# Routing that finds the group first and the two experts by a search of the eight largest, g2 spread by DMAs, and rms factors by one GpSimd power

## The chip, the core and the metric

The kernel runs on one core of a Trainium2 chip. The core has TensorE (PE in the profile; its weight loads are PEld), VectorE (DVE), ScalarE (ACT), GpSimd (POOL) and SyncE (SP), which issues most of the DMAs. Every engine works through its own queue of instructions in order. Data lie in HBM, in SBUF (128 partitions) and, for the results of TensorE, in PSUM. The metric is device time in microseconds (us), as the median of several runs; the profile is one further execution.

## What is computed

Two transformer blocks on 256 tokens of width 1024, in float32. The change lies in the first block's mixture of experts and in the factor of every rms norm; the second block (latent attention, gated linear attention, memory attention, a feed-forward part) it touches through that factor alone.

```python
def rms_norm(x, eps=NORM_EPS):
    y = xf * lax.rsqrt(jnp.mean(xf * xf, axis=-1, keepdims=True) + eps)

def hier_moe(h, w_group, b_group, w_router, b_router, w13, w2):
    """Top-1 expert group, then top-2 SwiGLU experts within it. h (b, s, d)."""
    g_logits = (hf @ w_group + b_group).astype(jnp.float32)
    g_prob = jax.nn.softmax(g_logits, axis=-1)
    p_g, g_idx = lax.top_k(g_prob, 1)
    e_logits = (hf @ w_router + b_router)....reshape(T, N_EXPERT_GROUPS, EXPERTS_PER_GROUP)
    within = jnp.take_along_axis(e_logits, g_idx[:, :, None], axis=1)[:, 0]
    top_v, top_i = lax.top_k(within, TOP_K)
    gate = p_g * jax.nn.softmax(top_v, axis=-1)
    expert_id = (g_idx * EXPERTS_PER_GROUP + top_i).astype(jnp.int32)
    ...   # y = sum over the token's two experts of gate * (silu(a) * b) @ w2[e], [a, b] = h @ w13[e]

sh1, sc1, g1, sh2, sc2, g2 = jnp.split(silu(c) @ w_ada + b_ada, 6, axis=-1)
x = x + g1 * mixer(modulate(x, sh1, sc1))
x = x + g2 * hier_moe(modulate(x, sh2, sc2))   # modulate: rms_norm(x) * (1 + scale) + shift
```

There are 4 groups of 8 experts, each with w13 of 1024x1024 and w2 of 512x1024, 6 MB of float32 weights an expert.

## The kernel before

Block 1's first part (`phase_a`) keeps the state transposed, xT, features on partitions. `ada_part` makes the 48 modulation columns `mod` in three parts of four weight loads each: four matmuls with 32 equal columns leave the result on four groups of 32 partitions, a copy takes it to `ada`, and four transposes turn it. `mod[:, 40:48]` is g2 as columns. At the end of the mixer, features 0 to 7 of x1T (the sum x + g1·mix, in tiles of 128) are made one after the other, squared on ScalarE and added up on VectorE; two matmuls with a column of ones give the tokens' sums `ss`, `rsqrt_cols` makes r2 of it, and L is the 36 router logits times r2 plus a bias.

`rsqrt` (lines 123 to 136) computes v^-0.5 on VectorE: a bit shift and an integer operation for a first guess, v times -0.5, and three Newton steps of three operations (L133 to L135); with the sum's scaling (L120) 13 operations at a site. Thirteen sites call it.

`routing` is a generator. Its first part transposes x1T into token rows (L695, tiles mm), scales them by r2 on ScalarE as `tm` and rounded as `h2h` (L699, L700), subtracts on GpSimd for the rest `h2l` (L701), and has `moe_start` put x1T into the four PSUM tiles of the result by sixteen transposes (L882). Then VectorE searches: `first_max` (L713 to L719) finds the first largest of the last axis, for all four groups at once (128x64), once more with the first one masked out (wi), and over the four groups (128x8); M (128x2x32, L733) marks a token's two experts. Matmuls with M give the experts' counts and ranks: pc (L736, L738) and, with a triangle and ones, the ranks of four experts (`ranks`, L744 to L747). Two groups of four matmuls (L757) and two copies on ScalarE (L760) spread g2 over all 128 partitions as `g2row`. The later parts of the generator, run under the first pass, transpose M (L768), sort the experts by their counts into P (L772 to L784), bring M, the counts and the gates G into that order (L788 to L792, L836 to L843), and compute the gates (L810 to L832).

`phase_b` goes through 32 experts in 11 passes: six with two experts, five with four. For two passes at a time `onehot` (L1003) makes the selecting matrix from the ranks, `gather` (L910) collects h2's rows by matmuls with h2h and h2l, and VectorE (L916) and ScalarE (L919) apply scale sc2 and shift sh2. `experts` then does w13 in eight k steps (L937, two PSUM tiles pa and pb), the gate by tanh and two products (L962 to L964), transposes (L967), w2 (L977), and adds the result, times gate and g2row (L984), to the result's tiles (L991). In the first pass a step of `routing` runs after each k step from the third on. The transposes of oh and matmuls with G (L948, L950) stand behind the k steps. Weights come by SP into ring buffers (`ring`, 2 MB) and `xb`; a buffer is given back when its matmuls are done (`done`), and SP's next load into it waits for that. The first four experts' weights do not depend on the routing.

Large matmuls of the other parts are done in three products of rounded halves: ScalarE rounds a weight (whi, L111), VectorE or GpSimd subtracts for the rest (wlo, L115 and L113).

The order on PE, DVE, ACT and POOL is that of a scheduler that goes through the program with a model of time; `tc.issue_after(x)` holds what follows behind instruction x. SP's order is that of the code.

## Time and profile before

| | |
|---|---|
| median of 3 runs | 1133.19 us (lowest 1131.82) |
| profiled execution | 1135.8 us, span 1134.0 us |
| busy share of the span | PE 93%, DVE 49%, ACT 39%, POOL 17% |
| HBM read | 324.57 MB, 287 GB/s over the span |

A row of the timeline gives start and duration in us, the engine, the line, the operation, output <- inputs by the program's names (numbers left out), partitions x elements, and the count of equal neighbours; behind it in brackets the engine's idle time ahead of it and what ended it. A group row gives busy us and mean ns of one, then idle time ahead and its releasers. A row of the waits gives total us, times and longest. A PE row often counts two records for one float32 matmul. The granted clock of PE is a share of 2.4 GHz.

### The profile page before, as it was taken

Reading aid. Unit: us, or ns where it says so; the run is one execution under the profiler, and the core shown is the slowest. Engines: PE = TensorE matmul, PEld = TensorE weight load, DVE = VectorE, ACT = ScalarE, POOL = GpSimd, SP = SyncE. Lnnn points to the kernel's source line nnn. Section 1 sums busy time; section 2 is a strip of 40 time slices with the busy share of each in tenths; the row PEclk is TensorE's granted clock in tenths of the full one; section 3 lists DMA queues with packets and bytes.
Section 4 is the critical chain, followed back from the end, with each engine's and each line's share of the span. In section 5 each row is a group of like instructions: output and inputs, shape, how many; then the busy total and the mean of one; then the engine's idle time right before and its main releaser. Section 6 shows DMA issues by size and latency. Waiting matters only on the chain. (4 is left out here: it accounts for less than half of the span.)

```text
span 1134.0 us, 18448 instructions
## 1 busy us (share of the span) xinstructions
PE 1055.1 (93%) x6921; PEld 714.0 (63%) x6921; DVE 554.7 (49%) x1355; ACT 436.7 (39%) x982; POOL 189.3 (17%) x181
## 2 busy tenths in 40 slices
PE   4999998999999998877889999999999999999998
PEld 2677778534343332241224578888898888898997
DVE  4498756312121220020211588475896766664664
ACT  3354434101111120010101557566864555565653
POOL 1453112000000000000001432222111132222221
PEclk9999989899999999979999999999999999999999
DMA  9885669499999999999999844553442243554531
GB/s 369 331 334 222 274 260 387 159 419 388 421 421 419 420 374 422 421 417 421 421 420 421 333 159 151 214 186 124 177 150 75 75 167 140 214 205 167 223 149 38
DMA packets 36279, 314.38 MB, mean 277 GB/s; under 512 B 4160, under 2 KB 4672, under 8 KB 5328
## 3 DMA queue, kind: packets, MB, share of 16 engines
q1 hardware_dynamic: 36176, 313.05, 69.0%
q8 instruction: 59, 0.97, 0.3%
q14 instruction: 44, 0.36, 0.1%
HBM read 324.57 MB, written 1.05 MB: 287 GB/s over the span
## 5 line engine op out<-in xcount | busy, mean ns | idle before, releaser
L111 ACT ACTIVATE whi<-ring 128x512 fp32r<-128x512 f32 (+3 forms) x378 | 228.6, 613 | 194.4 <-PE mm L175 94.6
L115 DVE TENSOR_TENSOR wlo<-ring,whi 128x512 fp32r<-128x512 f32 (+3 forms) x262 | 185.6, 711 | 131.6 <-ACT whi L111 119.8
L113 POOL TENSOR_TENSOR wlo<-ring,whi 128x512 fp32r<-128x512 f32 (+2 forms) x116 | 152.3, 1317 | 495.7 <-ACT whi L111 469.4
L937 PE MATMUL pb<-xb,xT 128*32 128x512 f32 x736 | 132.9, 595 | 7.4 <-DMA xb<-w 7.4
L937 PE MATMUL pb<-ring,xT 128*32 128x512 f32 x672 | 119.5, 595 | 5.3 <-DMA ring<-w 5.3
L963 DVE SCALAR_TENSOR_TENSOR g<-g,pb 128x256 f32<-128x256 f32 x22 | 9.3, 421 | 169.3 <-ACT g L962 169.3
L977 PE MATMUL pb<-xb,hT 128*32 128x512 f32 x464 | 84.8, 630 | 3.2 <-DMA xb<-w 2.7
L937 PEld LDWEIGHTS pb<-xb,xT 128*32 128x32 f32 x736 | 36.4, 109 | 81.0 <-issue 59.0
L962 ACT ACTIVATE g<-pb 128x256 f32<-128x256 f32 x22 | 8.4, 384 | 173.9 <-PE pb L937 168.6
L175 PE MATMUL mm<-h_lo,whi 128*128 128x256 f32 (+1 forms) x264 | 75.4, 286 | 0.0
L174 PE MATMUL mm<-h_hi,whi 128*128 128x256 f32 (+1 forms) x264 | 75.1, 285 | 0.0
L176 PE MATMUL mm<-h_hi,wlo 128*128 128x256 f32 (+1 forms) x264 | 75.1, 285 | 0.0
L113 POOL TENSOR_TENSOR ml<-ring,mh 128x256 fp32r<-128x256 f32 x8 | 5.6, 726 | 400.1 <-ACT mh L111 400.1
L175 PE MATMUL mm<-xg_lo,whi 128*128 128x256 f32 x256 | 71.2, 280 | 0.9 <-DVE xg_lo L1115 0.9
L174 PE MATMUL mm<-xg_hi,whi 128*128 128x256 f32 x256 | 70.7, 280 | 0.6 <-DVE xg_lo L1115 0.6
L176 PE MATMUL mm<-xg_hi,wlo 128*128 128x256 f32 x256 | 70.9, 279 | 0.0
L937 PEld LDWEIGHTS pb<-ring,xT 128*32 128x32 f32 x672 | 29.3, 109 | 65.0 <-issue 48.3
L984 DVE SCALAR_TENSOR_TENSOR Y<-pb,gs,g2row 128x512 f32<-128x512 f32 x22 | 16.5, 749 | 85.7 <-PE pb L977 84.8
L187 PE MATMUL mm<-whi,h_hi 128*128 128x512 f32 (+2 forms) x144 | 53.3, 374 | 0.6 <-issue 0.5
L188 PE MATMUL mm<-whi,h_lo 128*128 128x512 f32 (+2 forms) x144 | 53.3, 372 | 0.0
L977 PE MATMUL pb<-ring,hT 128*32 128x512 f32 x240 | 49.2, 618 | 3.4 <-ACT hT L968 1.9
L977 PEld LDWEIGHTS pb<-xb,hT 128*32 128x32 f32 x464 | 21.3, 114 | 48.4 <-issue 37.6
(530 smaller groups left out, 2245.3 us busy)
## 6 DMA issues: line engine op xcount, KB each, us to landing
xb<-w SPq DMA_DIRECT2D x110, 1024.0 KB, 15.6
ring<-w SPq DMA_DIRECT2D x82, 1024.0 KB, 13.3
ring<-w_in SPq DMA_DIRECT2D x18, 2048.0 KB, 8.4
ring<-w_ada SPq DMA_DIRECT2D x12, 2048.0 KB, 13.4
ring<-w_up SPq DMA_DIRECT2D x8, 2048.0 KB, 7.4
ring<-w_down SPq DMA_DIRECT2D x8, 2048.0 KB
ring<-w_out SPq DMA_DIRECT2D x2, 2048.0 KB, 11.9
ring<-w_mem_kv SPq DMA_DIRECT2D x2, 2048.0 KB
```

Source lines behind the costliest of these rows:

```text
L111: self.nc.scalar.activation(hi, src, AF.Copy)
L113: self.nc.gpsimd.tensor_tensor(out=lo, in0=src, in1=hi.bitcast(F32), op=OP.subtract)
L115: self.nc.vector.tensor_tensor(out=lo, in0=src, in1=hi.bitcast(F32), op=OP.subtract)
L174: nc.tensor.matmul(out, hv[:, k], xh[:, k0 + k], start=f, stop=False)
L175: nc.tensor.matmul(out, hv[:, k], xl[:, k0 + k], start=False, stop=False)
L176: nc.tensor.matmul(out, lv[:, k], xh[:, k0 + k], start=False, stop=l)
L187: nc.tensor.matmul(out[t], xh[:, k, s], hv[:, 0], start=f, stop=False)
L188: nc.tensor.matmul(out[t], xl[:, k, s], hv[:, 0], start=False, stop=False)
L937: nc.tensor.matmul(q[r, :], x[:, k, r], w[side[i]][:, h * 512:h * 512 + 512], start=k == 0, stop=k == KT - 1)
L963: nc.vector.scalar_tensor_tensor(g[:, r], g[:, r], 1.0, pa[:, r], op0=OP.add, op1=OP.mult)
L977: nc.tensor.matmul(y[h][r, :], hT[:, f * 128 + i * 32:f * 128 + i * 32 + 32], w[side[i]][:, h * 512:h * 512 + 512], start=f == 0, stop=f == 3)
L984: nc.vector.scalar_tensor_tensor(Y, y[h], gs, self.g2row[:, h * 512:h * 512 + 512], op0=OP.mult, op1=OP.mult)
```

## The change

Six parts. (1) `rsqrt` is one GpSimd power with a column of -0.5. (2) g2row: the bias part of g2 is loaded by SP from a new input `b_last` (128x512, each of four rows 32 times) into the left half of g2row; `ada_part` adds it to the last part's matmul result instead of copying, and eight DMAs from ACT's queue, 32x512 each, spread that tile over g2row; L757 and L760 are gone. (3) The search takes the group first, masks the logits of the other groups, and lets VectorE's max (the eight largest) and max_index find both experts; oq marks them, M is its sum. (4) The last square is kept apart (sq7), four matmuls add both tiles. (5) The h2l subtractions move to VectorE, half of them behind M (`found`), half behind the first gathers (`evac`). (6) `moe_start` and `gather` are generators: ten of the sixteen transposes stand early, six behind the rank matmuls; two of the four groups of gathers stand before the first pass, the others and all steps of `routing`, now with pc and the matmuls of oh and G, between its k steps.

```diff
     def rsqrt(self, pool, v, n):
         nc = self.nc
-        i = pool.tile([128, n], I32, tag=f"rq_i{n}", name=self.name("rqi"))
-        nc.vector.tensor_scalar(i, v.bitcast(I32), 1, None, op0=OP.arith_shift_right)
         y = pool.tile([128, n], F32, tag=self.name("rqy"), bufs=1, name=self.name("rqy"))
-        nc.vector.tensor_scalar(y.bitcast(I32), i, -1, 0x5F3759DF, op0=OP.mult, op1=OP.add)
...
-        for _ in range(3):
-            nc.vector.tensor_tensor(out=t, in0=y, in1=y, op=OP.mult)
-            nc.vector.tensor_tensor(out=t, in0=t, in1=w, op=OP.mult)
-            nc.vector.scalar_tensor_tensor(y, t, 1.5, y, op0=OP.add, op1=OP.mult)
+        nc.gpsimd.tensor_tensor(out=y, in0=v, in1=self.mhalf.to_broadcast([128, n]), op=OP.pow)
         return y
...
+            elif i == 2:
+                nc.sync.dma_start(out=self.g2row[:, 0:512], in_=a["b_last"])
...
-            if p:
+            if p == 2:
+                nc.vector.tensor_tensor(out=st, in0=ps, in1=self.g2row[:, 0:512], op=OP.add)
+                for i in range(2):
+                    for r in range(0, 128, 32):
+                        nc.scalar.dma_start(out=self.g2row[r:r + 32, i * 512:i * 512 + 512],
+                                            in_=st[64 + 32 * i:96 + 32 * i])
+            elif p:
                 nc.vector.tensor_copy(st, ps)
...
+            elif m == KT - 1:
+                nc.scalar.activation(sq7, x1T[:, m], AF.Square)
+                logits(m - 1)
...
-            self.last = nc.tensor.matmul(ss[:, t:t + 1], sq1[:, t * 128:t * 128 + 128], self.ones, start=True,
-                                         stop=True)
+            for s, q in enumerate((sq1, sq7)):
+                self.last = nc.tensor.matmul(ss[:, t:t + 1], q[:, t * 128:t * 128 + 128], self.ones, start=s == 0,
+                                             stop=s == 1)
...
-                nc.gpsimd.tensor_tensor(out=self.h2l[:, t, s_], in0=tm, in1=self.h2h[:, t, s_].bitcast(F32),
-                                        op=OP.subtract)
+                lows.append((self.h2l[:, t, s_], tm, self.h2h[:, t, s_]))
         with tc.issue_after(self.last.ins):
-            self.moe_start()
+            starts = self.moe_start()
+            for _ in range(10):
+                next(starts)
...
-        oh1, v1 = first_max(el, (2, 4, 8), d8)
-        wi2 = sb.tile([128, 2, 4, 8], F32, name="wi2")
-        nc.vector.scalar_tensor_tensor(wi2, oh1, -3.0e38, el, op0=OP.mult, op1=OP.add)
-        oh2, v2 = first_max(wi2, (2, 4, 8), d8)
-        ohg, gm = first_max(gl, (2, 4), self.desc[:, None, 4:8].to_broadcast([128, 2, 4]))
...
+        nc.vector.tensor_reduce(gm, gl, axis=AX.X, op=OP.max)
+        nc.vector.tensor_tensor(out=ohg, in0=gl, in1=b4(gm), op=OP.is_equal)
+        nc.vector.tensor_tensor(out=ohg, in0=ohg, in1=d4, op=OP.mult)
+        nc.vector.tensor_reduce(gk, ohg, axis=AX.X, op=OP.max)
+        nc.vector.tensor_tensor(out=ohg, in0=ohg, in1=b4(gk), op=OP.is_equal)
+        nc.vector.tensor_scalar(ohg, ohg, 3.0e38, -3.0e38, op0=OP.mult, op1=OP.add)
+        nc.vector.tensor_tensor(out=em.rearrange("p t (g e) -> p t g e", e=8), in0=el,
+                                in1=ohg[:, :, :, None].to_broadcast([128, 2, 4, 8]), op=OP.add)
...
+            nc.vector.max(v8[:, t], em[:, t])
+            nc.vector.max_index(i8[:, t], v8[:, t], em[:, t])
...
+        nc.vector.tensor_tensor(out=oq, in0=i8[:, :, 0:2, None].to_broadcast([128, 2, 2, 32]),
+                                in1=self.iota[:, None, None, 0:32].to_broadcast([128, 2, 2, 32]), op=OP.is_equal)
+        found = nc.vector.tensor_tensor(out=M, in0=oq[:, :, 0], in1=oq[:, :, 1], op=OP.add)
+        with tc.issue_after(found.ins):
+            for lo, tm, hi in lows[:2]:
+                nc.vector.tensor_tensor(out=lo, in0=tm, in1=hi.bitcast(F32), op=OP.subtract)
...
-        for j in range(2):
-            p = self.pst("aux")
-            with tc.issue_after(self.rank.ins):
-                for i in range(4):
-                    nc.tensor.matmul(p[:, i * 128:i * 128 + 128],
-                                     mod[:, 40 + j * 4 + i:41 + j * 4 + i].to_broadcast([128, 128]),
-                                     self.ident, start=True, stop=True)
-            nc.scalar.activation(self.g2row[:, j * 512:j * 512 + 512], p, AF.Copy)
+        with tc.issue_after(self.rank.ins):
+            for _ in starts:
+                pass
+        yield
...
             for k in range(KT):
+                if step:
+                    next(step, None)
...
-                if step and k > 1:
-                    next(step, None)
...
+        def first(rt):
+            next(ga)
+            next(ga)
+            next(rt)
+            yield
+            for k, _ in enumerate(rt):
+                if k % 2:
+                    next(ga, None)
+                yield
```

What stands in PE's queue from the end of the mixer to the first gather, first before the change: x1T's transposes (L882 moe, L695 mm), then everything that waits for M (`aux` are small PSUM tiles, `pb` a gather's).

```order
L882 MATMUL moe_2180<-ident,xT 128x128 x4
L882 MATMUL moe_2182<-ident,xT 128x128 x4
L695 MATMUL mm_2170<-ident,xT 128x128 x4
L736 MATMUL aux_2228<-ones,M 32x1 x2
L738 MATMUL aux_2228<-M,ones 32x32 x2
L744 MATMUL aux_2234<-M,stri 128x4
L745 MATMUL aux_2234<-M,ones 128x4
L746 MATMUL aux_2234<-M,stri 128x4
L757 MATMUL aux_2239<-ident,mod 128x128 x4
L757 MATMUL aux_2245<-ident,mod 128x128 x4
L910 MATMUL pb_2258<-oh_2253,h2h 128x256 x2
L910 MATMUL pb_2258<-oh_2253,h2l 128x256 x2
```

After it, the same place:

```order
L887 MATMUL moe_2147<-ident,xT 128x128 x4
L887 MATMUL moe_2149<-ident,xT 128x128 x4
L887 MATMUL moe_2148<-ident,xT 128x128 x2
L708 MATMUL mm_2131<-ident,xT 128x128 x4
L708 MATMUL mm_2139<-ident,xT 128x128 x4
L751 MATMUL aux_2185<-M,stri 128x4
L752 MATMUL aux_2185<-M,ones 128x4
L753 MATMUL aux_2185<-M,stri 128x4
L887 MATMUL moe_2148<-ident,xT 128x128 x2
L887 MATMUL moe_2150<-ident,xT 128x128 x4
L916 MATMUL pb_2203<-oh_2196,h2h 128x256 x2
L916 MATMUL pb_2203<-oh_2196,h2l 128x256 x2
```

pc and both L757 groups are gone from between M and the gather, and six transposes stand there instead.

PE in the first pass after the change, from the first k step (`pb` of L946 are pa and pb) on; before, all 16 gather rows stood ahead of the first k step, and L736 and L738 ahead of those:

```order
L946 MATMUL pb_2201<-ring_65,xT 32x512 x4
L946 MATMUL pb_2202<-ring_65,xT 32x512 x4
L772 MATMUL aux_2235<-ones,M 32x1 x2
L774 MATMUL aux_2235<-M,ones 32x32 x2
L946 MATMUL pb_2201<-ring_65,xT 32x512 x4
L946 MATMUL pb_2202<-ring_65,xT 32x512
L778 MATMUL aux_2240<-ident,M 32x128 x2
L946 MATMUL pb_2202<-ring_65,xT 32x512 x3
L946 MATMUL pb_2201<-ring_63,xT 32x512 x4
L946 MATMUL pb_2202<-ring_63,xT 32x512 x4
L946 MATMUL pb_2201<-ring_63,xT 32x512 x4
...
L798 MATMUL aux_2268<-P,MT 128x32 x2
L800 MATMUL aux_2268<-P,ic 1x32 x2
L916 MATMUL pb_2275<-oh_2196,h2h 128x256 x2
```

pc, the transposes of M, the matmuls with P and the second half of the gathers stand between k steps now.

VectorE at the end of the search, up to the ranks R of the first four experts (m, k and oh are first_max's, v and i in the second piece the eight largest and their indices); before:

```order
L719 TENSOR_TENSOR oh_2201<-oh_2201,k_2204 128x64
L719 TENSOR_TENSOR oh_2219<-oh_2219,k_2222 128x8
L726 SCALAR_TENSOR_TENSOR wi_2207<-oh_2201,L 128x64
L713 TENSOR_REDUCE m_2209<-wi_2207 128x8
L715 TENSOR_TENSOR oh_2211<-wi_2207,m_2209 128x64
L716 TENSOR_TENSOR oh_2211<-oh_2211,cst 128x64
L718 TENSOR_REDUCE k_2214<-oh_2211 128x8
L719 TENSOR_TENSOR oh_2211<-oh_2211,k_2214 128x64
L732 TENSOR_TENSOR M<-oh_2201,oh_2211 128x64
L733 TENSOR_TENSOR M<-M,oh_2219 128x64
L747 SCALAR_TENSOR_TENSOR R_2233<-aux_2234,M 128x8
L763 COPY sh_81<-mod 128x8
```

and after:

```order
L730 TENSOR_TENSOR ohg<-ohg,gk 128x8
L731 TENSOR_SCALAR ohg<-ohg 128x8
L732 TENSOR_TENSOR em<-L,ohg 128x64
L737 MAX v_2172<-em 128x8 x2
L738 MAX_INDEX i_2173<-v_2172,em 128x8 x2
L825 TENSOR_TENSOR dv_2311<-v_2172 128x2
L740 TENSOR_TENSOR oq<-i_2173,cst 128x128
L823 TENSOR_REDUCE pg_2309<-ge 128x2
L743 TENSOR_TENSOR M<-oq 128x64
L746 TENSOR_TENSOR h2l<-tm_2120,h2h 128x512
L746 TENSOR_TENSOR h2l<-tm_2128,h2h 128x512
L754 SCALAR_TENSOR_TENSOR R_2184<-aux_2185,M 128x8
```

The second wide search (L726 to L719) is gone, max and max_index stand in its place behind the group's search, and two h2l subtractions have come between M and R.

## Rows read from the trace of the kernel before

**Rows 1.** Stretches: length; busy PE, PEld, DVE, ACT, POOL (count); PE clock; DMA share; GB/s.

```profile
200.00:205.00 5.00, 4.65 (x27) 4.62 (x28) 2.03 (x16) 0.70 (x2) 0.00 (x0) 0.50 0.01 3
230.00:235.00 5.00, 5.00 (x36) 1.30 (x32) 0.00 (x0) 0.00 (x0) 0.00 (x0) 0.73 1.01 419
395.00:400.00 5.00, 5.00 (x37) 2.14 (x39) 1.79 (x10) 1.67 (x2) 0.00 (x0) 1.00 0.72 298
400.00:600.00 200.00, 166.69 (x830) 56.25 (x826) 29.40 (x87) 19.01 (x40) 0.77 (x2) 0.95 1.01 417
660.00:670.00 10.00, 7.81 (x32) 6.08 (x31) 9.64 (x23) 3.32 (x8) 3.09 (x2) 0.83 0.18 60
800.00:850.00 50.00, 49.93 (x349) 45.44 (x348) 46.23 (x144) 35.86 (x112) 9.71 (x7) 1.00 0.46 169
```

**Rows 2.** Waits between 190 and 230 us, PE's only long one.

```profile
PE aux L736 <- DVE M L733: 4.8, 1, 4.8
```

**Rows 3.** Timeline: the factor r2, its first operation and its first user.

```profile
190.19 0.16 DVE L120 TENSOR_SCALAR rqv<-aux 128x2 f32<-128x2 f32 x1 [0.76 <-PE aux L674]
192.56 0.42 DVE L679 SCALAR_TENSOR_TENSOR L<-aux,rqy,br 128x36 f32<-128x36 f32 x2
```

**Rows 4.** Timeline: the search, with GpSimd's subtractions beside it.

```profile
193.96 2.49 POOL L701 TENSOR_TENSOR h2l<-tm,h2h 128x512 fp32r<-128x512 f32 x2 [10.57 <-ACT h2h L700]
196.90 1.05 DVE L715 TENSOR_TENSOR oh<-wi,m 128x64 f32<-128x64 f32 x1
199.46 0.22 DVE L719 TENSOR_TENSOR oh<-oh,k 128x64 f32<-128x64 f32 x1
199.98 0.23 DVE L733 TENSOR_TENSOR M<-M,oh 128x64 f32<-128x64 f32 x1
```

**Rows 5.** Timeline: from M to the first gather.

```profile
200.35 0.35 PE L736 MATMUL aux<-ones,M 128*32 128x1 f32 x4 [4.82 <-DVE M L733]
202.19 3.54 PE L757 MATMUL aux<-ident,mod 128*128 128x128 f32 x16
202.66 0.88 DVE L1003 TENSOR_TENSOR oh<-iota,R 128x128 fp32r<-128x128 f32 x4
205.49 0.49 PE L910 MATMUL pb<-oh,h2h 128*128 128x256 f32 x2
```

**Rows 6.** Timeline: the first pass.

```profile
209.49 5.36 PE L937 MATMUL pb<-ring,xT 128*32 128x512 f32 x48
214.78 0.11 PEld L768 LDWEIGHTS aux<-ident,M 128*32 128x32 f32 x2 [0.84 <-issue]
225.87 0.63 PE L842 MATMUL aux<-P,GT 32*128 32x32 f32 x4
228.59 8.77 PE L977 MATMUL pb<-xb,hT 128*32 128x512 f32 x64
```

**Rows 7.** Groups of instructions: GpSimd's and VectorE's prices.

```profile
L701 POOL TENSOR_TENSOR h2l<-tm,h2h 128x512 fp32r<-128x512 f32 x4 | 5.0, 1266 | 10.7 <-ACT h2h L700 10.7
L398 POOL TENSOR_TENSOR pool_c<-pool_c,ident 128x128 f32<-128x128 f32 x8 | 4.6, 593 | 0.0
L115 DVE TENSOR_TENSOR wlo<-ring,whi 128x512 fp32r<-128x512 f32 (+3 forms) x262 | 185.6, 711 | 131.6 <-ACT whi L111 119.8
```

**Rows 8.** Timeline: places in the first 190 us.

```profile
12.20 0.16 DVE L120 TENSOR_SCALAR rqv<-aux 128x2 f32<-128x2 f32 x1 [1.17 <-PE aux L268]
15.66 1.22 PE L203 MATMUL aux<-ident,rqy 128*128 128x128 f32 x4
15.79 0.33 SPq L104 DMA_DIRECT2D ring<-w_ada  x1
25.11 2.96 POOL L113 TENSOR_TENSOR wlo<-ring,whi 128x512 fp32r<-128x512 f32 x2 [23.06 <-ACT whi L111]
152.56 0.38 ACT L615 ACTIVATE pl<-aux 128x256 f32<-128x256 f32 x1 [3.88 <-PE aux L613]
```

**Rows 9.** Timeline: PE in the second block.

```profile
662.81 1.22 PE L189 MATMUL mm<-wlo,mh 128*128 128x512 f32 x2 [2.19 <-DVE wlo L115]
```

More of the change, by code (lines that the diff above doesn't have):

```diff
@@ L654, in phase_a @@
         sq1 = sb.tile([128, T], F32, name="sq1")
+        sq7 = sb.tile([128, T], F32, name="sq7")
         for m in range(KT):
@@ L689, in routing @@
         self.h2l = self.act.tile([128, 2, D], F32R, tag="hl", name="h2l")
-        for t in range(2):
-            for j in range(2):
+        lows = []
+        for j in range(2):
+            for t in range(2):
                 pt = self.pst("mm")
@@ L731, in routing @@
-        Mg = M.rearrange("p t (g e) -> p t g e", e=8)
-        nc.vector.tensor_tensor(out=Mg, in0=oh1, in1=oh2, op=OP.add)
-        nc.vector.tensor_tensor(out=Mg, in0=Mg, in1=ob, op=OP.mult)
-        pc = self.pst("aux")
-        for t in range(2):
-            nc.tensor.matmul(pc[0:32, 0:1], M[:, t], self.ones, start=t == 0, stop=t == 1)
-        for t in range(2):
-            nc.tensor.matmul(pc[0:32, 32:64], self.ones.to_broadcast([128, 32]), M[:, t], start=t == 0,
-                             stop=t == 1)
+        gm, gk = [sb.tile([128, 2], F32, name=n) for n in ("gm", "gk")]
@@ L936, in experts @@
                                 r = slice(i * 32, i * 32 + 32)
[L937 to L938 removed]
+                                self.used = nc.tensor.matmul(
+                                    q[r, :], x[:, k, r], w[side[i]][:, h * 512:h * 512 + 512],
+                                    start=k == 0, stop=k == KT - 1)
                 if k % 2:
                     w13.done(k // 2)
[L941 to L942 removed]
             if between:
@@ L1056, in more @@
             onehot(oh, self.R, first, (64, 64), io)
-            gather(xs[:, 0:1], oh)
+            for _ in gather(xs[:, 0:1], oh):
+                pass
             experts(first, xs[:, 0], oh, (64, 64), Late("w13", first), Late("w2", first), turns=((0,), (1,)))
@@ L1079, in phase_b @@
                 nc.sync.dma_start(out=self.fw, in_=a["final_row"].to_broadcast([128, D]))
+            if p == 0:
+                rt = first(rt)
             if p % 2 == 0:
@@ L1086, in phase_b @@
                 n = len(both)
-                gather(xs[:, 0:n], oh[:, :, 0:n].rearrange("p t e s -> p t (e s)"))
+                ga = gather(xs[:, 0:n], oh[:, :, 0:n].rearrange("p t e s -> p t (e s)"))
+                if p:
+                    for _ in ga:
+                        pass
             q = p % 2
```

73 lines of the change are left out of this document (37 added, 36 removed).

## The prediction

> **What bounds the kernel now.** I read four views. First the busy time by stretch, to see which resource is full where [rows 1]; the reader is to compare the DMA share with PE's busy time. From 400 to 600 us the DMA engines are full (share 1.01) and PE is busy for 167 of 200 us; from 800 to 850 PE is busy for 49.93 of 50 us. At 395 to 400 the share falls to 0.72 while PE is full: every buffer holds a weight that PE has not used, so SP waits for PE to give one back, and PE's place in the expert passes sets when the later transfers start. Second the waits between 190 and 230 us, the stretch of the routing [rows 2]: PE waits once for long, 4.8 us for M, and for no DMA. Third the timeline of that stretch, instruction by instruction [rows 3 to 6]. Fourth the prices of the other engines' operations [rows 7]. The reading: from the end of block 1's mixer to the start of the first pass's w2 matmuls (228.59, [rows 6]) the time is one chain of small dependent steps, and a shift S of that point moves the rest of the kernel with it, because behind it PE, then the transfers that PE releases, then PE again set the pace.
>
> **Change, part a: the rms factor.** From the start of rqv (190.19) to that of L (192.56) twelve VectorE operations take 2.37 us, 0.2 each [rows 3]. One stays (rqv); 2.2 us become one GpSimd power, d, and two hops between engines of 0.1 to 0.15 (M's end at 200.21 to L736 at 200.35, [rows 4, 5]). The trace has no power. Bounds for d: 0.16, a VectorE operation of the same shape [rows 3], and 1.27, a GpSimd subtraction of 256 times as many elements [rows 7]. I take 0.7, near the 0.59 of a 128x128 GpSimd operation [rows 7] and a little over it, because a power is more work per element than a sum. Part a saves 2.2 - 0.7 - 0.2, so 1.3 (0.7 to 1.8). The other twelve sites sit beside other work: the first is needed by PE at 15.66, behind matmuls, 3.3 us after rqv is done [rows 8]; in the second block PE is full. If that cover is gone, each costs what it is late.
>
> The Trainium skill, "GPSIMD Engine Reference", section 4.1, Engine selection, speaks against this part: it puts elementwise work with two inputs on VectorE, as about twice as slow on GpSimd. By it d would be twice a VectorE operation of 0.16, an estimate of 0.32, and part a would save 1.7; the trace's subtraction of 128x512 is 1.27 on GpSimd against 0.71 on VectorE [rows 7], so the factor agrees at that size.
>
> **Part b: the search.** From L's end (192.98, [rows 3]) to M's end (200.21, [rows 4]) 7.2 us pass. While GpSimd's two pairs of h2l subtractions run (from 193.96, 2.49 us a pair), a 128x64 VectorE operation takes 1.05 instead of 0.22 [rows 4]. After the change VectorE runs thirteen operations on the path (two reductions, two comparisons, a product, a scalar operation, em, two maxima, two index searches, oq, M) and three that slip in between (ge, dv, pg; the order shows them): 16, and no GpSimd subtraction stands beside them. At 0.2 each [rows 3], 3.2 us. Maxima and indices do not occur in the trace; bounds for one: 0.16, and 0.44, twice a 128x64 operation [rows 4]; so the search takes 2.8 to 4.4, and part b saves 4.0 (2.8 to 4.4).
>
> **Part c: from M to the first gather.** 200.21 to 205.49 is 5.3 us now [rows 4, 5]: the matmuls of pc and of the ranks until 202.19, then sixteen L757 rows of 3.54 together, 0.22 each, at a granted clock of 0.50, which is 1.2 GHz [rows 1], after PE had stood idle for 4.8 us. After the change a pair of h2l subtractions (2 x 0.71, [rows 7]) runs on VectorE beside the rank matmuls, then R (0.2), four one-hots (0.88, [rows 5]) and hops: 2.95. PE's six transposes stand beside these. Part c saves 2.3. If PE still runs at 1.2 GHz, its own work binds: six rank matmul rows, 1.4, and twelve rows of 0.22 for six transposes, 2.7, with a hop 4.3; then it saves 1.0. By parts a and b PE's idle time ahead of M shrinks from 4.8 to under 1 us, hence I take the full clock.
>
> **Part d: from the gather to the w2 matmuls.** 205.49 to 228.59 is 23.1 us [rows 5, 6]. Into the first pass goes what stood before or behind it: the matmuls of pc (0.5), L842 (0.63, [rows 6]), and the six of oh and G, for which I take half as much again, 0.9: 2.0. PE changes between expert matmuls and small ones four times more; between nothing and the 0.84 for which the weight load of L768 waits for issue [rows 6] I take 0.3 each, 1.2. In return the tail ahead of w2 no longer holds L842 and its followers, and w2 begins behind the first pair of transposes: 0.9. Net loss 2.3 (1 to 4). The change also shortens the links of the chain that runs under this pass: a k step is 0.9 us (48 L937 rows, eight a step, take 5.36), and one or two steps stand between two links, where from L736 to L768 there were 14 us [rows 5, 6].
>
> **Part e: what is moved into the first 190 us.** b_last is 0.25 MB, 0.6 us at the 417 GB/s of [rows 1], with one issue on SP of 0.33 [rows 8]. Eight DMAs on ACT's queue, at the same 0.33 some 2.6 us, stand ahead of pl, and there ACT waits 3.88 us for PE [rows 8]. Sum 0; if that cover is gone, 2.6. The eight transposes and two matmuls that now stand ahead of the factor are PE work taken from behind it, and an addition falls away: 0.
>
> **Part f: the second block.** PE waits 2.2 us for wlo at 662.81 [rows 9], and VectorE is behind with factors and products there. VectorE loses eleven operations at a site, but the products stay ahead of that wlo. I take 0.5 (0 to 4: the wait, and 1.7 at the clock of 0.83, [rows 1]).
>
> Sum: 1.3 + 4.0 + 2.3 - 2.3 = 5.3 (S), and 0.5: 5.8. The profiled execution took 1135.8 (its span is 1134.0, and 1.8 lies around it), so 1130.0; it is 2.6 above the median of the runs, 1133.2, hence 1127.4, rounded to 1127.5.
>
> **Rivals.** (A) The gain is lost again under the first pass: a link of the chain comes late, and PE, which runs in order, stands behind it. Against it: each link has 0.9 us or more. For it: between L772 and L798 VectorE holds the other pair of h2l (1.4, [rows 7]), evacuations of the gather, and kr, rk and P, seven operations of 0.2, beside three k steps; two links late by 1.5 us take 3 of the 5.3. Gain 0 to 2.5: 1130.7 to 1133.2.
> (B) More than 10 us: the clock of 0.73 at 230 to 235 (1.4 us, [rows 1]) and all of part f's 3.9 go too, 5.3 + 1.4 + 3.9: 1122.6, and with a cheap power and a short search down to 1120. For it: fewer VectorE operations there; against: the same products ahead of wlo.
> (C) Slower, by the power itself: S is 2.2 - 0.2 - d + 4.0 + 2.3 - 2.3, that is 6.0 - d, and below zero from d = 6.0 on; from there a power also stands in GpSimd's queue ahead of wlo in the second block, where PE is full and waits for wlo [rows 1, 9]. At d = 12, S is -6, and two sites late by 3 us bring 1145. For it: no power in the trace; against: GpSimd's rows at these sizes are all below 1.3 [rows 7].
> (D) The first power alone is late, because its code has to arrive: up to 3.3 us are covered [rows 8]; at twice that, 3.3 of the 5.8 are lost: 1130.8. Against it: GpSimd's first subtraction at 25.11 waited for ACT's whi alone [rows 8]. The Trainium skill, "GPSIMD Engine Reference", section 2.1, Instruction dispatch, states about 6 us for the first call of newly loaded code; by that figure an estimate of 2.7 is lost and the time is 1130. No row before shows such a load.
>
> **Chances.** My forecast 0.62, A 0.15, B 0.10, C 0.06, D 0.07. The forecast's own range, from the ends of its parts: S from 2.5 to 8, f up to 2: 1123 to 1131. The range takes in A, D and most of B: 1120.5 to 1133.5, and leaves out C and the far end of B. Two per cent is 22.7 us, about what a measurement of this kernel can tell from no change: faster needs under 1110.5, for which two thirds of the 36 us from L to w2 would have to go (0.01); slower needs over 1155.9, which only C at many sites reaches (0.03); the rest is within 2% (0.96).
>
> **What would show it.** After the change: at r2 one GpSimd power under 1.3 us and L one hop behind it; 128x64 operations at 0.2 and M about 5 us earlier; a granted clock near 1.0 between M and the gather; the first w2 matmul of the first pass at 223; the same offset at 400, 600 and the end. I am wrong if PE waits inside the first pass, if the offset at 228 is not kept at 600, or if a power takes over 3 us.

## The result: 7 us slower, and the profile after

| | before | after |
|---|---|---|
| median of 20 runs each, us | 1134.08 | 1141.14 |
| profiled execution / span, us | 1135.8 / 1134.0 | 1141.2 / 1139.4 |
| PE busy, us | 1055.1 (93%) | 1057.9 (93%) |

The ratio is 1.0062, interval 1.0052 to 1.0072: 7 us slower where 1127.5 was forecast, and outside the range. Two of before's 20 runs took 1204 and 1669 us; without them its median is 1133.5. The two profiled executions are 5.4 us apart, and most single executions lie within 5 us of the median of their kernel; so below, traces tell where something happens, and ratios of runs tell how much it is worth (0.1% is 1.1 us). An offset is the start of an instruction in one trace less that of the same instruction in the trace before.

The stretches after, columns as in [rows 1]; the two first have no counterpart there, so the first one before the change follows:

```profile
155.00:160.00 5.00, 2.27 (x12) 1.16 (x10) 0.96 (x5) 0.00 (x0) 1.64 (x1) 0.50 1.00 352
160.00:165.00 5.00, 3.67 (x15) 2.31 (x16) 0.48 (x1) 1.24 (x3) 0.00 (x0) 0.50 0.93 305
200.00:205.00 5.00, 3.91 (x35) 3.70 (x35) 4.54 (x25) 4.89 (x10) 0.08 (x1) 1.00 0.80 333
400.00:600.00 200.00, 165.58 (x825) 53.30 (x825) 28.63 (x83) 18.82 (x36) 0.70 (x1) 0.93 0.99 412
660.00:670.00 10.00, 9.35 (x46) 7.50 (x45) 9.07 (x11) 5.35 (x10) 7.11 (x5) 1.00 0.49 198
```

```profile
155.00:160.00 5.00, 5.00 (x44) 3.87 (x42) 1.69 (x5) 1.42 (x4) 0.00 (x0) 0.74 0.65 275
```

From 155 to 165 PE is idle for 4 of 10 us; before, it was busy for all of 155 to 160. The waits of PE after (total, times, longest) say for whom:

```profile
PE aux L622 <- ACT pl L620: 4.1, 1, 4.1
PE aux L751 <- DVE M L743: 1.1, 1, 1.1
PE mm L178 <- PEq L1495: 2.7, 1, 2.7
PE mm L180 <- DVE wlo L115: 1.2, 2, 0.7
```

The second answers [rows 2]: the wait for M fell from 4.8 to 1.1, as meant. The first is new: L622 are the matmuls with pl, and pl is what ACT makes behind the eight DMAs. The third is PE at the branch in line 1495, also new. The fourth answers [rows 9]: there the longest wait was 2.2.

ACT's queue and PE at the first of these waits; the row with ACTq is the eight DMAs from issue to issue:

```profile
153.29 7.56 ACTq L295 DMA_DIRECT2D g2row<-ada  x8
160.90 0.38 ACT L620 ACTIVATE pl<-aux 128x256 f32<-128x256 f32 x1 [7.79 <-DMA g2row<-ada]
161.33 1.22 PE L622 MATMUL aux<-pl,pool_c 128*128 128x256 f32 x2 [4.06 <-ACT pl L620]
```

The first seven of the eight are issued 0.65 apart, until 157.78. The eighth stands for 2.5 us more. Why is told by the semaphores of the instructions in the trace: SP's and ACT's DMAs use eight of them in turn, and the eighth waits on that of a weight load of 1 MB which SP had issued at 152.45. The two rows, the load and the eighth:

```profile
152.45 0.33 SPq L864 DMA_DIRECT2D ring<-w  x1
160.31 0.54 ACTq L295 DMA_DIRECT2D g2row<-ada  x1
```

The load lands at 160.29, 7.84 after its issue, and the eighth DMA starts 0.02 later.

The pl that starts at 160.90 stood at 152.56 before [rows 8]: 8.3 later, of which 4.7 were already there at 140 us. The chain of the routing after, to be read against [rows 3 to 6]:

```profile
199.14 0.16 DVE L120 TENSOR_SCALAR rqv<-aux 128x2 f32<-128x2 f32 x1 [2.03 <-PE aux L686]
199.38 0.70 POOL L126 TENSOR_TENSOR rqy<-rqv,mhalf 128x2 f32<-128x2 f32 x1 [7.44 <-DVE rqv L120]
200.11 0.42 DVE L691 SCALAR_TENSOR_TENSOR L<-aux,rqy,br 128x36 f32<-128x36 f32 x2 [0.82 <-POOL rqy L126]
202.02 0.29 DVE L737 MAX8 v<-em 128x8 f32<-128x32 f32 x2
202.33 0.19 DVE L738 FIND_INDEX8 i<-v,em 128x8 uint32<-128x32 f32 x1
203.04 0.22 DVE L743 TENSOR_TENSOR M<-oq 128x64 f32<-128x64 f32 x1
205.69 0.47 PE L916 MATMUL pb<-oh,h2h 128*128 128x256 f32 x2
231.83 3.63 PE L985 MATMUL pb<-xb,hT 128*32 128x512 f32 x28 [0.53 <-ACT hT L976]
```

The chain starts 8.95 late (199.14 against 190.19) and ends 3.24 late (231.83 against 228.59): it gained 5.7. So the step that was forecast with most care came true, and the kernel is slower because the chain starts 9 us late.

### The profile page after: what moved, and what is told of

The parts are those of the page before. It is cut to its first block, busy times and chain, and to the rows that moved or that the text cites. A ratio compares the mean times of both kernels' runs of the same rounds, so it can differ in the third digit from the quotient of the medians.

```text
span 1139.4 us, 18296 instructions
## 1 busy us (share of the span) xinstructions
PE 1057.9 (93%) x6909; PEld 708.4 (62%) x6909; DVE 532.3 (47%) x1196; ACT 435.4 (38%) x980; POOL 198.6 (17%) x191
## 5 line engine op out<-in xcount | busy, mean ns | idle before, releaser
L115 DVE TENSOR_TENSOR wlo<-ring,whi 128x512 fp32r<-128x512 f32 (+3 forms) x262 | 182.0, 699 | 135.6 <-ACT whi L111 123.3
L113 POOL TENSOR_TENSOR wlo<-ring,whi 128x512 fp32r<-128x512 f32 (+2 forms) x116 | 147.6, 1277 | 459.0 <-ACT whi L111 438.5
L946 PE MATMUL pb<-xb,xT 128*32 128x512 f32 x736 | 135.4, 596 | 7.1 <-DMA xb<-w 6.9
L946 PE MATMUL pb<-ring,xT 128*32 128x512 f32 x672 | 120.0, 595 | 5.2 <-DMA ring<-w 5.2
L126 POOL TENSOR_TENSOR rqy<-rqv,mhalf 128x2 f32<-128x2 f32 (+3 forms) x12 | 20.6, 1713 | 393.5 <-DVE rqv L120 393.5
L946 PEld LDWEIGHTS pb<-xb,xT 128*32 128x32 f32 x736 | 35.1, 109 | 79.6 <-issue 57.8
L946 PEld LDWEIGHTS pb<-ring,xT 128*32 128x32 f32 x672 | 29.6, 109 | 65.1 <-issue 49.0
L985 PE MATMUL pb<-ring,hT 128*32 128x512 f32 x240 | 52.4, 639 | 2.7 <-ACT hT L976 2.2
```

The source lines that it names most:

```text
L113: self.nc.gpsimd.tensor_tensor(out=lo, in0=src, in1=hi.bitcast(F32), op=OP.subtract)
L115: self.nc.vector.tensor_tensor(out=lo, in0=src, in1=hi.bitcast(F32), op=OP.subtract)
L126: nc.gpsimd.tensor_tensor(out=y, in0=v, in1=self.mhalf.to_broadcast([128, n]), op=OP.pow)
L946: self.used = nc.tensor.matmul(q[r, :], x[:, k, r], w[side[i]][:, h * 512:h * 512 + 512], start=k == 0, stop=k == KT - 1)
L985: nc.tensor.matmul(y[h][r, :], hT[:, f * 128 + i * 32:f * 128 + i * 32 + 32], w[side[i]][:, h * 512:h * 512 + 512], start=f == 0, stop=f == 3)
```

## The experiments

All ratios are to before's runs of the same comparison, with intervals of 95%.

| kernel | what it has of the change | ratio | interval |
|---|---|---|---|
| e7_power_alone | powers | 1.0006 | 0.9997 to 1.0016 |
| f3_routing_alone | routing, old rsqrt, g2 by matmuls | 0.9974 | 0.9961 to 0.9987 |
| e6_matmul_tiles | routing and powers, g2 by matmuls | 0.9972 | 0.9959 to 0.9985 |
| e8_b_last | e6 and the load of b_last | 1.0001 | 0.9986 to 1.0016 |
| e2_tiles | all, old scratch tiles kept | 1.0041 | 1.0027 to 1.0055 |
| after | all | 1.0062 | 1.0052 to 1.0072 |
| f4_g2_alone | b_last and eight DMAs only | 1.0042 | 1.0027 to 1.0056 |

From the third row to the sixth the kernels differ by one thing each: b_last costs 0.0029 (3.3 us), the DMAs in place of the matmuls 0.0040 (4.5), the scratch tiles 0.0021 (2.4). Each of these is uncertain by about 2 us (the runs of e8_b_last lie between 1127.9 and 1134.9), so each is looked up in the traces too.

### Where the DMAs stand: e1_spread, e5_sp_queue

e1_spread issues the eight DMAs behind the squares of features 0 to 3, where ACT was thought to have room; e5_sp_queue puts them on SP's queue.

```diff
 e1_spread, behind the square of each feature m < 4:
+            for i in range(2 * (m < 4)):
+                with tc.issue_after(done.ins):
+                    nc.scalar.dma_start(out=self.g2row[m * 32:m * 32 + 32, i * 512:i * 512 + 512], ...)
 e5_sp_queue:
-                        nc.scalar.dma_start(out=self.g2row[r:r + 32, ...
+                        nc.sync.dma_start(out=self.g2row[r:r + 32, ...
```

> The changed kernel with the eight g2row DMAs moved: they stand on ACT's queue behind the squares of features 0 to 3, two behind each, instead of between ada and pl; nothing else differs. Theory (the DMAs block ACT): in the trace of the changed kernel they occupy ACT's queue for 7.56 us from 153.29, pl starts at 160.90 and PE waits 4.1 us for it, part of it made up by slower work later. Then pl comes about 4 us earlier, PE waits under 1 us there, and the kernel is 3 to 4.5 us faster than the changed one as a whole: about 1137. Rival 1 (the loss before 190 us is the clock: longer stretches at 1.2 GHz at 22, 49, 114 and 155 us): pl early, but the time within 1 us of the changed kernel, 1140.5. Rival 2 (the DMAs cost the same wherever they stand, by slowing ACT's roundings): PE waits for whi between 176 and 190 and the time stays.

> The changed kernel with the eight g2row DMAs issued from SP's queue instead of ACT's, at the same place in the program (in SP's queue between the second and the third load of expert weights); nothing else differs. Theory (the DMAs block the engine that issues them, 0.65 us each and once a wait of 3 us): ACT is free, pl follows its matmuls within 1 us, PE's wait of 4.1 us and its clock of 0.50 from 155 to 165 us go; SP is blocked instead, and the expert loads behind it, which end some 5 us before their first matmul in the changed kernel, still come in time. 3 to 5 us faster than the changed kernel: 1.002 to 1.004 of before. Rival (SP's delay reaches the first pass, or b_last and the shared order of the transfers is what costs): 1.005 or more.

e1_spread: 1143.82, ratio 1.0091 (1.0076 to 1.0106), slower still: a miss. pl was early (its matmuls start at 156.64 instead of 161.33), but the DMAs now held up roundings. The timeline of ACT and PE in e1_spread, and ACT's longest wait there for a DMA:

```profile
176.28 7.03 ACTq L681 DMA_DIRECT2D g2row<-ada  x2
186.49 2.19 ACT L111 ACTIVATE whi<-ring 128x512 fp32r<-128x512 f32 x4 [2.67 <-issue]
187.17 0.58 PE L165 MATMUL mm<-mxh,whi 128*128 128x256 f32 x1 [7.18 <-ACT whi L111]
ACT sq L676 <- DMA xb<-w: 8.7, 1, 8.7
```

Two DMAs take 7.03 from issue to issue, four roundings of weights pile up behind them, and PE waits 7.18 for the first. 6.0 of the 7.03 are again the wait for a weight load (xb) that SP had issued. So the cost is not tied to pl, and ACT had no free place behind the squares either.

e5_sp_queue: 1135.13, ratio 1.0015 (1.0002 to 1.0028), 5.3 us better than after. Its SP row, SP's wait ahead of the eighth DMA, and its stretch from 155 on:

```profile
151.67 7.70 SPq L295 DMA_DIRECT2D g2row<-ada  x8
SPq L295 <- DMA ring<-w: 2.8, 1, 2.8
155.00:160.00 5.00, 4.96 (x48) 3.62 (x50) 1.85 (x5) 1.81 (x5) 0.19 (x1) 1.00 0.80 236
```

On SP the eight take 7.70, no less than on ACT: 0.64 from one issue to the next, and the same stop ahead of the eighth, 2.8 us for a load of `ring` to land (2.5 in after). So the 0.64 belongs to this kind of DMA and not to the engine, and the stop belongs to the load whose semaphore the eighth shares. But PE waits for no load between 140 and 232 us in e5_sp_queue, it waits only 0.5 for pl, and the granted clock is 1.00 (2.4 GHz) where after has 0.50.

### No DMAs, no b_last: e4_g2_matmul, e6_matmul_tiles, e8_b_last, f4_g2_alone, g2_no_bias

e4_g2_matmul takes after and makes g2row as before, by L757 and L760. e6_matmul_tiles also keeps the scratch tiles of the old rsqrt. e8_b_last is e6 with the load of b_last, unused. f4_g2_alone is before with only the new g2row. g2_no_bias is after without b_last; it leaves out the bias of the last part of mod, sc2's too, so the routing is another and the time can't be read.

```diff
 e4_g2_matmul (against after)
-                nc.sync.dma_start(out=self.g2row[:, 0:512], in_=a["b_last"])
...
-                        nc.scalar.dma_start(out=self.g2row[r:r + 32, ...
...
+                    nc.tensor.matmul(p[:, i * 128:i * 128 + 128], mod[:, 40 + j * 4 + i:...
+            nc.scalar.activation(self.g2row[:, j * 512:j * 512 + 512], p, AF.Copy)
 e8_b_last (against e6_matmul_tiles)
+                nc.sync.dma_start(out=self.g2row[:, 0:512], in_=a["b_last"])
```

> The changed kernel with g2row made in the old way: eight matmuls and two ACT copies behind the rank matmuls, no b_last and no DMAs; search, powers and interleaving as changed. Theory (DMAs block ACT): 4 us come back ahead of 160 us, and about 2 us of matmuls return between the ranks and the first gather, of which the six transposes' place hides none: 1138 to 1139.5. Rival 1 (the loss before 190 us is the clock's): 1141 to 1143. Rival 2 (b_last's transfer between the first weight loads matters as well): the stretch from 20 to 125 us becomes 2 us shorter too, and the time is 1136 to 1137.

> The changed kernel with g2row made by eight matmuls as before (no b_last, no DMAs) and with the unused scratch tiles of the old rsqrt kept, so that uh and ul have their old distance to the weights. Theory (the two edits add, since they act at different places): the g2 matmuls gave 0.9977 of before, the tiles 2.2 to 2.4 us; 0.9977 - 0.0020, so 0.9955 to 0.9962, 1127.5 to 1128.5. Rival (the tiles' effect in the changed kernel was of another cause): 0.9975.

> As the run with the g2 matmuls and the kept tiles, plus the load of b_last into g2row, at the place that it has in the changed kernel; its data are not used (g2row is written over later). Theory (0.25 MB between the first weight loads are 0.6 us, and the loads have slack): within 0.7 us of that run. Rival (the 3 us that the changed kernel loses between 85 and 125 us against the one with g2 matmuls are b_last's, through a ring load that comes late for ada's matmuls): 2 to 3 us slower than that run.

> The kernel before with the g2 part as its only change: b_last, eight DMAs on ACT's queue, no g2 matmuls and copies. Theory (this part is what made the changed kernel slower): about 3 us by b_last and the longer stretches at 1.2 GHz, 4 to 5 by the DMAs in front of pl, less 1 to 3.5 us for the matmuls that go from the routing: 1.003 to 1.007. Rival (the loss needs the other parts, through the scheduler's order): 0.998 to 1.001.

> The changed kernel without b_last: ada's last part is copied instead of added, so the bias of g2 is left out of the result; the eight DMAs stay on ACT's queue. It tells b_last's share of the loss from that of the DMAs. Theory (b_last's load moves ada's weight loads and by that PE's order between 80 and 125 us, 3 us; the DMAs on ACT's queue cost 5): 1.0025 to 1.0045 of before. Rival 1 (b_last alone is nothing, its run differed by the clock): 1.0055 to 1.0070. Rival 2 (without b_last the DMAs wait less for their turn and ACT is free earlier): below 1.002.

e4_g2_matmul: 1130.31, ratio 0.9977 (0.9966 to 0.9988), 8 us better than expected, which first showed that part e of the prediction, put at nothing, was the whole loss. e6_matmul_tiles: 1129.42, 0.9972, where 0.9955 to 0.9962 was expected. e8_b_last: 1133.27, 1.0001: the load alone costs 3.3 us against e6_matmul_tiles, near the rival's 2 to 3. f4_g2_alone: 1138.30, 1.0042: both together cost 4.8 net of the two groups of matmuls that they replace. Of g2_no_bias (1439.97, ratio 1.2707) only the first 190 us can be used: its offset is +1.3 at 130 and +5.5 at 168, so the DMAs on ACT cost 4.2 there without b_last too.

How a quarter of a megabyte costs 3.3 us: SP's queue after, then PE's part of the modulation around 122 us in e6_matmul_tiles and in e8_b_last:

```profile
4.45 0.46 SPq L104 DMA_DIRECT2D ring<-w_ada  x1
4.96 0.45 SPq L224 DMA_DIRECT2D g2row<-b_last  x1
15.30 0.33 SPq L104 DMA_DIRECT2D ring<-w_ada  x1
87.52 0.33 SPq L104 DMA_DIRECT2D ring<-w_in  x1
```

```profile
121.05 1.92 PE L282 MATMUL mm<-ring,silc 128*32 128x512 f32 x16
```

```profile
122.79 1.05 PE L286 MATMUL mm<-ring,silc 128*32 128x512 f32 x2
124.31 1.06 PE L286 MATMUL mm<-ring,silc 128*32 128x512 f32 x6
125.87 1.06 PE L286 MATMUL mm<-ring,silc 128*32 128x512 f32 x8
```

The stretch around them in e6_matmul_tiles, in e8_b_last, and in f1_whole_gather (described below), which has no b_last:

```profile
112.00:124.00 12.00, 11.93 (x69) 7.54 (x69) 8.55 (x22) 5.27 (x11) 1.28 (x1) 0.86 0.71 302
112.00:124.00 12.00, 12.00 (x51) 8.55 (x50) 8.26 (x18) 4.04 (x8) 1.27 (x1) 0.72 0.84 356
112.00:124.00 12.00, 12.00 (x63) 7.78 (x63) 7.30 (x19) 4.57 (x10) 1.28 (x1) 0.73 0.64 270
```

The 0.25 MB themselves are not seen. But the scheduler's order on PE is another with b_last: the modulation's matmuls that stood at 80.94 before come 4.5 later and SP's load of w_in with them (87.52 against 83.70), and at 122 they stand in pieces between other matmuls, so that sixteen of them, once 1.92 in one row, take 3.17. At 130 us the seven kernels with b_last have offsets of +3.0 to +4.9, the eight without it +0.1 to +1.5. From 110 to 130 us alone the seven lose 2.6 to 3.8, and seven of the eight less than 0.1. The eighth, f1_whole_gather, has its sixteen in one row and still loses 1.6: its granted clock from 112 to 124 is 0.73, near the 0.65 to 0.72 of the kernels with b_last, where the others have 0.86. So about 1.6 of the loss goes with the lower clock, and the pieces, 1.25 longer, make up most of the rest. That the order, and not the transfer, is the cause of both is read from the traces; a kernel with b_last and the old order was not tried, and why the clock is lower is open.

### The power: e3_newton, e7_power_alone, f2_newton16

e3_newton is after with the old rsqrt at all thirteen sites; e7_power_alone is before with the powers; f2_newton16 is e6 with the old rsqrt at the sites with 16 columns only.

```diff
 f2_newton16 (against e6_matmul_tiles)
-        nc.gpsimd.tensor_tensor(out=y, in0=v, in1=self.mhalf.to_broadcast([128, n]), op=OP.pow)
+        if n < 16:
+            nc.gpsimd.tensor_tensor(out=y, in0=v, in1=self.mhalf.to_broadcast([128, n]), op=OP.pow)
+            return y
+        ...   # the old three Newton steps
```

> The changed kernel with the old rsqrt (twelve VectorE operations) at all thirteen sites, the rest as changed. Theory (the power saves at r2 and its GpSimd time of 0.7 to 3.3 us costs elsewhere little): at r2 L comes 1.3 to 1.5 us later, the stretch from 655 to 700 us loses the 3 to 4 us that the changed kernel gained there, and the tiles' addresses give back 2 us: 1140.5 to 1143. Rival (the powers are what made the kernel slower: 1.4 to 3.3 us each where twelve VectorE operations take 2.4, in GpSimd's queue ahead of weight subtractions): 1134 to 1138.

> The kernel before with the GpSimd power at all thirteen sites as its only change, the old scratch tiles kept. Theory (a power of 0.7 us at r2 saves 1.3 us there; 655 to 700 us gains 2 to 4; the branch behind 777 us, whose code comes 3 us later in the profiles with powers, takes 2 to 3 back): 0.997 to 0.9995 of before. Rival 1 (the powers cost, as the pair with and without them in the changed kernel suggests, 1.6 us slower with): 1.001 to 1.003. Rival 2 (nothing, all hidden): 0.9995 to 1.0005.

> As the run with g2 by matmuls and the kept tiles, but the three sites with 16 columns use the old twelve VectorE operations instead of a power of 3.0 us. Theory (the branch behind 777 us is late because, with the powers, the 2 MB weight load is issued ahead of the branch's code fetch instead of behind it): the order of the two at that place is that of the kernel before, the branch takes 3.6 us again instead of 6.8, and the time is 2 to 3 us lower than that run: 0.9945 to 0.9955. Rival (the branch's delay does not hang on the 16-column powers, or the gain at 655 to 700 us goes with them): 0.9970 to 0.9985.

e3_newton: 1136.23, ratio 1.0027 (1.0015 to 1.0038), 1.6 better than e2_tiles, its like with powers, where 2.5 to 5 more was expected: a miss. Its trace is 3.0 later than that of e2_tiles at 340 us and 5.2 earlier at 400; that stretch is looked at under the sum below. e7_power_alone: 1133.53, 1.0006: the powers by themselves are worth nothing. Yet e7's trace is 2.0 early at 240 us and gains 3.1 more between 640 and 680; 3.7 are given back at 780. The place of that is the branch of line 1495 (1469 before). ACT behind it, in before, after, e3_newton and f2_newton16:

```profile
780.72 1.68 ACT L111 ACTIVATE whi<-ring 128x512 fp32r<-128x512 f32 x3 [2.86 <-ACTq L1469]
```

```profile
784.86 1.68 ACT L111 ACTIVATE whi<-ring 128x512 fp32r<-128x512 f32 x3 [6.49 <-ACTq L1495]
```

```profile
782.22 1.67 ACT L111 ACTIVATE whi<-ring 128x512 fp32r<-128x512 f32 x3 [2.70 <-ACTq L1504]
```

```profile
770.33 1.68 ACT L111 ACTIVATE whi<-ring 128x512 fp32r<-128x512 f32 x3 [2.39 <-ACTq L1501]
```

The branch takes 3.5 to 4.1 us in six kernels and 6.6 to 7.2 in nine. In each of the nine SP has issued a 2 MB load of w_in 0.60 to 0.62 us ahead of it; in each of the six that load is issued 0.02 behind it. What the engines wait for is their next code, which packets on two queues of their own bring: at 777.7 to 778.3 before, at 781.9 to 782.2 after. That they queue behind the load is the likely reading, and fits fifteen traces (all but g2_no_bias); the load was not moved by itself. The Trainium skill, "Runtime: NRT & Kernel Launch", section Instruction fetch mechanics, says that a taken branch whose target is not in the window of fetched code forces a DMA fetch before execution goes on. These rows agree; the page gives no time and says nothing of a load in front. f2_newton16 (1125.46, ratio 0.9930, 0.9917 to 0.9944, better than expected) shows that the powers with 16 columns bring the bad order: without them the branch is short again, and the ratio is 0.0042 (4.8 us) below e6's. Of that the traces put 1.8 between 760 and 960 us; where the rest lies is open.

The prices of the powers after, by shape (busy us, mean ns of one):

```profile
L126 POOL TENSOR_TENSOR rqy<-rqv,mhalf 128x16 f32<-128x16 f32 x3 | 9.1, 3023 | 7.5 <-DVE rqv L120 7.5
```

With 2 columns it is 0.70 (above), with 4 1.39, with 8 1.83, with 16 3.02 in the mean and 3.27 at most. On GpSimd the time grows with the columns, and most of the thirteen sites have more than r2's two.

### The scratch tiles: e2_tiles

The new rsqrt needs none of the old tiles i, w and t. e2_tiles declares them all the same, unused.

```diff
+        i = pool.tile([128, n], I32, tag=f"rq_i{n}", name=self.name("rqi"))
+        w = pool.tile([128, n], F32, tag=f"rq_w{n}", name=self.name("rqw"))
+        t = pool.tile([128, n], F32, tag=f"rq_t{n}", name=self.name("rqt"))
```

> The changed kernel with the three scratch tiles of the old rsqrt still allocated but not used; no instruction differs, only the SBUF addresses of what is allocated behind them (uh and ul of the feed-forward part move by 96 bytes). Theory (addresses): in the trace of the changed kernel a matmul of the feed-forward part with uh or ul takes 0.232 us where before took 0.227, over some 390 of them 2 us; with the old distance between uh and the weights the period is 0.227 again and the time 2 to 2.5 us lower than the changed kernel: about 1139. Rival (the period differs by chip or by run): 0.232 stays or differs in the run of before too, and the time is that of the changed kernel within 0.7 us.

1137.95, ratio 1.0041: 2.4 better than after by the ratios (3.2 by the medians), by a kernel that issues the same instructions. The two intervals overlap slightly, so the traces have to decide. Up to 960 us the traces lie within 0.5 of each other; the gain is in the feed-forward part. One of its groups in before, after and e2_tiles:

```profile
L187 PE MATMUL ff<-whi,uh 128*128 128x512 f32 x128 | 49.8, 389 | 0.0
```

```profile
L178 PE MATMUL ff<-whi,uh 128*128 128x512 f32 x128 | 50.7, 396 | 0.0
```

```profile
L181 PE MATMUL ff<-whi,uh 128*128 128x512 f32 x128 | 49.8, 389 | 0.0
```

Without the old tiles uh and ul lie 64 bytes lower than before and whi and wlo 32 bytes higher in each partition (against e2_tiles, uh and ul alone lie 96 lower), and the matmul that reads both is 7 ns longer; its three groups are busy for 141.9 instead of 139.7. Behind 960 us the five kernels without these tiles lose 2.3 to 2.4 against before, the ten others 0.1 or less. Which bits of the addresses matter was not tried. Between e4 and e6 the same tiles give 2.3 in the trace, but only 0.9 in the medians (1130.31 against 1129.42), with intervals that overlap.

### The routing: f3_routing_alone, f1_whole_gather, and both gains together: g1_both

f3_routing_alone is e4 with the old rsqrt. f1_whole_gather is e6 with all four groups of gathers ahead of the first pass. g1_both is f1 with the old rsqrt at the 16-column sites.

```diff
 f1_whole_gather (against e6_matmul_tiles)
             next(rt)
+            for _ in ga:
+                pass
             yield
-            for k, _ in enumerate(rt):
-                if k % 2:
-                    next(ga, None)
+            for _ in rt:
                 yield
```

> The search, the interleaving and the drop of the last addition alone: g2 by matmuls, the old rsqrt at every site. Theory (routing's parts b, c and d save 4 us net, of which the DMA bound up to 600 us keeps 2 to 4; the powers are neutral in sum, as their run alone showed): 0.996 to 0.998. Rival (the power at r2 is what lets the routing gain through): 0.9985 to 1.0005.

> As the run with g2 by matmuls and the kept tiles, but all four groups of gathers stand ahead of the first pass, as before the change; routing's steps stay between its k steps. Theory (the prediction's part d: each change between expert matmuls and small ones costs 0.3 to 0.5 us on PE, and nothing waits for the early start of the first pass): two changes fewer, and the first w2 matmul comes 0.5 to 1.5 us earlier; 0.9960 to 0.9970 of before. Rival (the second half's low parts, which VectorE subtracts only behind the first gathers, come too late for a gather that follows at once): PE waits 1 to 2 us ahead of the first pass and the time is 0.998 to 0.999.

> The three edits that each made the kernel faster, together: g2 by matmuls with the scratch tiles kept, all gathers ahead of the first pass, and the old rsqrt at the three sites with 16 columns. Theory (they act at different places: 207 to 231 us, and behind 700 us): the gather's 1.4 us and the branch's 2 us add: 0.9915 to 0.9930 of before, 1123 to 1125. Rival (behind 228 us the DMA engines set the pace to 600 us and take the gather's gain back): 0.9930 to 0.9940.

f3_routing_alone: 1130.43, ratio 0.9974: the routing is worth 3 us by itself. f1_whole_gather: 1126.67, 0.9941 (0.9927 to 0.9955), better than expected; from r2 (0.8 later than in e6) to the w2 matmuls (224.24 against 225.21) it gains 1.7, so spreading the gathers between k steps is a loss. g1_both: **1123.19, ratio 0.9916 (0.9902 to 0.9931)**, 9.5 us faster than before and the fastest of all. Its first w2 matmul stands 4.5 earlier than before's (224.10), its offset at 240 us is -6.2, and its branch is short:

```profile
767.43 1.67 ACT L111 ACTIVATE whi<-ring 128x512 fp32r<-128x512 f32 x3 [3.05 <-ACTq L1501]
```

## Why the prediction was wrong

**Part a was right.** rqv to L is 0.97 instead of 2.37; 1.4 saved, 1.3 forecast, with d at 0.70 exactly. (The 2.37 before were thirteen operations, not twelve, which changes nothing in the sum.) That the guess for d was exact is luck: it came from another operation with 64 times as many elements, and a power with four columns already takes 1.39. The rule that was weighed there (the Trainium skill, "GPSIMD Engine Reference", section 4.1, Engine selection: about twice as slow with two inputs) gave an estimate of 0.32; measured are 0.70 against 0.16 for a VectorE row of the same shape, a factor of four. For this operation at that size the rule was too kind to GpSimd; no power ran on VectorE.

**Part b was right.** L's end (200.53) to M's end (203.26) is 2.7 instead of 7.2; 4.5 saved, 4.0 forecast. The wide operations take 0.22 with no GpSimd subtraction beside them, and a maximum about 0.15.

**Part c was right.** M to the gather is 2.4 instead of 5.3; 2.9 saved, 2.3 forecast. The granted clock from 200 to 205 is 1.00 (2.4 GHz) where it was 0.50 (1.2 GHz).

**Part d was right, at a higher price.** Gather to w2 is 26.1 instead of 23.1; 3.0 lost, 2.3 forecast in 1 to 4. f1 shows that over half of it is the spreading of the gathers. Together S is 5.7, forecast 5.3. Rival A's place, the links under the first pass, shows no wait of PE over 0.2 us up to 230.

**Part e failed, and decides the result.** "Sum 0; if that cover is gone, 2.6" priced a DMA at 0.33 by a load on SP. Eight of these take 7.56 on ACT and 7.70 on SP: 0.64 apart, and a stop of 2.5 to 2.8 ahead of the eighth, until a weight load with the same semaphore has landed. Over the cover of 3.88 that is 3.7, and the traces of after, e2, e3, f4 and g2 show 3.7 to 4.2. Without the stop it would be 1.2, an estimate from the same rows. The "2.6" came from a row of another kind of transfer, from HBM instead of between partitions, and held no wait for other DMAs, so it was no upper bound. Also in part e, b_last was priced by its bytes and its issue (0.6 and 0.33). Its cost, 3.3, came with another order on PE and a lower clock around 120 us. The two together lose 7 us ahead of the routing, more than S. No rival held this: the moved DMAs had none of their own, and the only way to slower in the list was the power.

**Part f was wrong twice, both ways.** The wait for wlo fell as the bound allowed (0.5 forecast, 0 to 4): the offset falls by 3.1 from 660 to 668 and by 0.9 more up to 720, and the stretch from 660 to 670 has a clock of 1.00 instead of 0.83. In f3, with the old rsqrt, 2.2 fall there too, so it is not the power alone. But 2 to 3 come back at the branch, which no part of the sum spoke of, and 2.2 in the feed-forward part, by addresses.

**Rivals C and D are false.** The first power is not late: it takes 0.70 as that of r2 does, and the matmul that needs it starts at 15.16 instead of 15.66. The 6 us that the Trainium skill, "GPSIMD Engine Reference", section 2.1, Instruction dispatch, gives for the first call of newly loaded code show in no run here. The point that decided C was a d of 6.0; the largest power takes 3.27.

**The signs of being wrong.** PE does not wait inside the first pass, as said. But a power does take over 3 us, with 16 columns, and the offset is not kept: +2.9 at 340 us, +4.5 at 600.

**The sum with the measured terms**, as offsets in the trace after: +4.6 at 130 us (1.0 of it was there at 50 us, of either sign in other kernels and not explained; the rest came with b_last), +3.7 by the DMAs, +0.6 up to r2, -5.7 by S, +1.6 between 340 and 600, -4 from 660 to 720, +2 at the branch, +2.3 in the feed-forward part; it ends at +4.9.

The +1.6 is where the kernels differ most: after and e2_tiles lose 1.6 to 1.8 between 340 and 600 us, and the twelve others (g2_no_bias left out) gain 0.4 to 4.2. There the DMA engines are full (share 1.01), except around 400 us. That place in after and in e3_newton:

```profile
400.00:405.00 5.00, 5.00 (x42) 2.21 (x45) 2.71 (x15) 1.92 (x3) 0.00 (x0) 1.00 0.25 105
400.00:405.00 5.00, 5.00 (x52) 2.02 (x48) 0.00 (x0) 1.47 (x2) 0.00 (x0) 1.00 1.01 421
```

Before, the share falls to 0.72 from 395 to 400 [rows 1]; e2_tiles and e7_power_alone have such a hole too (0.30 and 0.48 in one stretch of 5 us), e1, e3, e4, e6, e8, f1, f2, f3 and g1 none. Why it comes in one kernel and not in another was not tried, so a part of the differences between kernels stays open here: of the 9.5 us between the traces of after and e4_g2_matmul, 5.2 stand at 340 us and 4.0 come up to 600.

## What to carry to other kernels

A DMA is priced by a row of its own kind, by what its issue may have to wait for, and by what its queue's engine does next: eight small transfers between partitions held ACT for 7.6 us, a third of it waiting for another engine's weight load, and the same eight on SP cost nothing that shows. A new load or a freed tile is not free because its bytes are few: it can change the scheduler's order and the addresses of all that follows, so one kernel that has only that edit, unused, is worth its run. Where several edits go together, the one put at nothing is to be tried alone first: here the change without it, with the 16-column powers undone and the gathers kept together, gives 0.9916, and the whole 1.0062.
